# Moving the pool means, their row sums and two scale pieces in the start of a hybrid decoder block

## The chip, the cores and the metric

The kernel runs on one core of a Trainium2 chip. The metric is the device time of one execution in microseconds (us), median of several runs. The engines work side by side, each through its own list of instructions in order: TensorE (PE, with its weight loads shown apart as PEld), VectorE (DVE), ScalarE (ACT), GpSimd (POOL) and SyncE (SP), which here only issues loads.

## The reference

One decoder layer over 1024 tokens of 1024 features. What the change touches is the first half of it:

```python
mod = jax.nn.silu(c) @ w_ada + b_ada
shift1, scale1, gate1, shift2, scale2, gate2 = [m[:, None, :] for m in jnp.split(mod, N_MOD, axis=-1)]
h = rms_norm(x, norm1_pre) * (1.0 + scale1) + shift1
z = h @ w_in
y_a = spatial_gating(z[..., : 2 * D_A], w_spatial, b_spatial, ln_v_gain, ln_v_bias)
y_b = multiscale_pool(z[..., 2 * D_A:], w_pool, b_pool, pool_scale)
mix = jnp.concatenate([y_a, y_b], axis=-1) @ w_out
x = x + gate1 * rms_norm(mix, norm1_post)
```

`multiscale_pool` takes, for each of four groups of 128 features, the mean of the last 2, 4, 8 or 16 tokens (of fewer at the start of the sequence, divided by their true count) minus the token itself, and multiplies the difference by a 128 x 128 matrix. A constant added to every token of a feature drops out of that difference. After this half comes an MLP with a squared ReLU.

## The kernel before

Products in full precision are made of reduced-precision parts (`hi` and `lo`, three products each); a few small ones run in plain float32, which takes two TensorE instructions each. Tokens go in two halves of 512 (h = 0, 1). `start()` does the first half as far as the inputs of the output projection. Its instructions stand in an order written out by hand on all five engines (`manual_schedule`, L1664); from `project` (L1673) to `project_last` a planner puts them in order by its own estimates, and may set them among those of `start()`; the MLP (`expand`, `contract`) is by hand again.

In `start()`, in order:

- **Normalising** (L1391 to L1411). For each of four tiles of 128 tokens: ScalarE squares and sums (`first`), GpSimd takes the power, VectorE scales (`second`), TensorE transposes three of eight feature blocks (`third`).
- **Scale.** The columns of `w_ada` for `scale1` come in five pieces, of 128, 128, 256, 256 and 256 columns. `piece_sum` (L1306) multiplies and adds the eight rows of a piece with `silu(c)` on VectorE into two accumulators, whose sum a ninth step (`both`, L1316) makes. `piece_end` (L1322) adds over the partitions by TensorE products with a column of ones, and `ada_vector` adds the bias on VectorE. The four pieces of `shift1` go the same way later.
- **Pool products** (`pool_pass`, L1417): z of the pool groups without the shift, into the PSUM tiles `pbs`, feature block after feature block; `scaled_hi`, `pool_hi` (ACT) and `scaled_lo`, `pool_lo` (DVE) make the operands. ScalarE copies the result to `zbs` (L1513).
- **Value products** (L1552 to L1586), with the shift pieces beside them. What the shift adds is computed from sums of the weights' rows, weighted by the shift: `row_sum` into `vacc` (value), `uacc` (gate) and `bacc` (pool).
- **Gate products** (`gate_pass`, L1591) with `sums_b` and `sums_u` beside them on VectorE, and the statistics of the values (`values`).
- **Tail** (L1631 to L1661). `row_vector(bacc)` gives the shift of the pool groups, which ScalarE adds to `zbs`; `windowed` (L379) makes the means from it on VectorE and saves the last 16 tokens in `halo` for the second half; `spatial_products`; `pool_out` (L415) multiplies by the pool matrix; `spatial_end` (L470) makes the four `ya`. `stream.fill(n)` takes the next unit of `w_out` (load `w_raw`, ACT `whi`, DVE `wlo`). `load_x(1)` loads the second half's tokens into the tiles that held the pool weights (`braw` is `xs[4]` to `xs[7]`), so each such load waits until `sums_b` has read its tile.

Then `project` (L552) needs the first unit of `w_out` and the first two pool results, four PSUM tiles for four tiles of tokens.

Of the kernel before, what the change touches and what calls it, by code (L numbers as in the profile page):

```python
# [40 lines left out]
def block_kernel(  # L41
# [64 lines left out]

    def load_x(h):
        for i in range(NT):
            nc.sync.dma_start(out=xs[h * NT + i], in_=x[0, (h * NT + i) * P:(h * NT + i + 1) * P, :])
# [9 lines left out]
    ident = const.tile([P, P], F32, name="ident")  # L119
    make_identity(nc, ident)  # L120
    ones = const.tile([P, P], F32, name="ones")
    nc.vector.memset(ones, 1.0)
# [347 lines left out]

    def spatial_end(h, j, ps, u):
        t = tmp.tile([P, NT, P], F32, tag="t", name=f"ya{h}_{j}")
        nc.vector.scalar_tensor_tensor(
            t, ps.rearrange("p (n t) -> p n t", t=P), vec[:, V_LG + j:V_LG + j + 1],
            Bsp[:, j:j + 1, :].broadcast_to([P, NT, P]), ALU.mult, ALU.add,
        )
        tf = t.rearrange("p n t -> p (n t)")
        nc.vector.tensor_tensor(tf, tf, u, ALU.mult)
        y = fact.tile([P, 2, HT], F32R, tag="f", name=f"yas{h}_{j}")
        split(y[:, 0], y[:, 1], tf)  # L480
        return y

# [823 lines left out]
    def piece_sum(blk, c0, n, ts):  # L1306

        def step(kt):
            def run():
                acc = acc_of[blk][kt % 2][:, c0:c0 + n]  # L1310
                if kt < 2:
                    nc.vector.tensor_scalar(acc, ts[kt], silu_c[:, kt:kt + 1], None, ALU.mult)
                else:
                    nc.vector.scalar_tensor_tensor(acc, ts[kt], silu_c[:, kt:kt + 1], acc, ALU.mult, ALU.add)
            return run
        def both():  # L1316
            a, b = [acc_of[blk][o][:, c0:c0 + n] for o in range(2)]
            nc.vector.tensor_tensor(a, a, b, ALU.add)

        return [step(kt) for kt in range(KT)] + [both]  # L1320

    def piece_end(blk, c0, n, split=False):  # L1322
        pa = ps_tile(f"pa{blk}_{c0}")
        nk = n // P
        for k in range(nk):
            at = c0 + k * P
            nc.tensor.matmul(pa[:, k:k + 1], lhsT=acc_of[blk][0][:, at:at + P], rhs=ones[:, 0:1], start=True, stop=True)
        rest = lambda: ada_vector(blk, pa[:, 0:nk], range(c0 // P, c0 // P + nk))
        return rest if split else rest()

# [8 lines left out]
    def start():  # L1339
# [50 lines left out]

        g = piece_sum(1, *PIECES[0], sc[0])  # L1391
        first(0)
        first(1)
        vectors_a()
        second(0)
        third(0)
        first(2)
        second(1)
        third(1)
        first(3)  # L1400
        second(2)
        third(2)
        weave(g)
        second(3)
        scale_rest = piece_end(1, *PIECES[0], split=True)
        third(3)
        scale_rest()
        for i in range(NT):
# [5 lines left out]
        hT = []  # L1414
        pbs = [ps_tile(f"pb0_{j}") for j in range(NG)]

# [16 lines left out]
        hT.append(scaled_hi(pts[0], 0))  # L1433
        g = piece_sum(1, *PIECES[1], sc[1])
        weave(g[:KT // 2])
        scaled_lo(hT[0], pts[0], 0)
        weave(g[KT // 2:])
        pool_lo(0)
        pool_pass(0, 0)
        pool_pass(0, 1)  # L1440
        piece_end(1, *PIECES[1])
        his(1)
        pool_pass(0, 2)
        more(3)
        g = piece_sum(1, *PIECES[2], sc[2])
        weave(g[:KT // 2])
# [17 lines left out]
        def value_hi(kp):  # L1464
            nc.scalar.copy(vw[kp][0], vraw[kp])
# [39 lines left out]
        value_lo(0, 0)  # L1505
        value_lo(0, 1)
        pool_pass(KT - 1, 1)
        pool_pass(KT - 1, 2)
# [10 lines left out]

        bacc, vacc, uacc = rows_of("b"), rows_of("v"), accp.tile([P, 512], F32, tag="junk", bufs=1, name="shift_wu")  # L1520

# [30 lines left out]
        for kp in range(NQ):  # L1552
            if kp == 0:
                sh.append(piece(0, 2 * QC, QC))
                value_tiles(1)
                value_hi(1)
# [25 lines left out]
            if kp == 1:  # L1582
                rest_b()
                turn()
            if kp == 2:
                offsets()  # L1586


# [24 lines left out]
        for i in range(NT):  # L1613
            nc.tensor.matmul(pvs[i], lhsT=ones_r, rhs=vb[:, 0], start=False, stop=False)
            nc.tensor.matmul(pvs[i], lhsT=ones_r, rhs=vb[:, 1], start=False, stop=True)
        weave(sums_b(0, 4), sums_u(0, 2))
        gate_load(3)
        gate_pass(2)
        gate_pass(3)
        steps, vs = values(0, pvs)  # L1620
        weave(steps[:4], sums_b(4, 8))
        gate_hi(2)
        gate_lo(2, 0)
        gate_lo(2, 1)
        gate_pass(4)
        weave(steps[4:], sums_u(2, 6))
# [24 lines left out]
        ya = []  # L1651
        for j in range(NHEAD):
            if j in (1, 2):
                stream.fill(1 + j)
            ya.append(spatial_end(0, j, psp[j], us[j]))
            if j < 2:
                yb[2 + j][1]()
            if j == 2:
                measure()
        apply()  # L1660
        return ya + [y for y, low in yb]  # L1661


    with tc.manual_schedule(engines={E.DVE, E.Activation, E.PE, E.Pool, E.SP}):  # L1664
        y0 = start()
    nxt = {}

    def prepare(key, h, n, name):
        def run():
            nxt[key] = hidden(h, n, name)  # L1670
        return run
# [38 lines left out]
```

## Time and profile before

| | us |
|---|---|
| median of 3 runs | 917.52 |
| lowest, highest | 917.51, 918.11 |
| profiled execution | 918.05 |
| its span, first to last instruction | 916.4 |

TensorE is busy for 97% of the span, VectorE for 75%, ScalarE for 46%, GpSimd for 10%. The profile says for each engine when it worked, what it waited for, and which clock TensorE was granted (1.0 is the upper of two levels). It lists no clock before the first change that it recorded, and shows 1.0 there.

### The profile page before, as it was taken

How to read it: one execution, taken by the hardware profiler on the slowest of the kernel's cores; microseconds unless marked ns; L12 is line 12 of the kernel's file. 1: busy time of each engine (PE TensorE's matmuls, PEld its weight loads, DVE VectorE, ACT ScalarE, POOL GpSimd, SP SyncE). 2: the span in 40 equal slices, each digit the busy share in tenths (PEclk: the TensorE clock that was granted, in tenths of full speed). 3: DMA queues.
4: the chain of work that ended last, by engine and by line, in shares of the span. 5: the costliest groups of instructions: out<-in, count | busy, mean ns of one | idle time of the engine just before them, and what ended most of it. 6: DMA issues, size and time to landing. Idle time of an engine off the chain costs nothing.

```text
span 916.4 us, 10781 instructions
## 1 busy us (share of the span) xinstructions
PE 888.7 (97%) x3960; PEld 723.9 (79%) x3960; DVE 687.5 (75%) x980; ACT 419.1 (46%) x558; POOL 88.8 (10%) x147
## 2 busy tenths in 40 slices
PE   4999999999999999999999999999999999999994
PEld 3788678888887888888888888888888888888883
DVE  5988878799758997766666656477987774569796
ACT  3323675334366665444444354454455433434331
POOL 4001020003003001111100101010000000000032
PEclk9999999999999999999999999999999999999997
DMA  9934356584824159533444434499975884334664
GB/s 309 352 111 149 98 149 199 160 271 151 254 81 151 41 142 303 184 138 132 168 149 157 141 138 148 139 358 392 354 239 196 291 271 123 107 114 139 208 213 153
DMA packets 114105, 173.52 MB, mean 189 GB/s; under 512 B 6098, under 2 KB 61442, under 8 KB 114052
## 3 DMA queue, kind: packets, MB, share of 16 engines
q1 hardware_dynamic: 104292, 135.03, 46.0%
q0 software_dynamic: 9760, 37.80, 10.7%
q8 instruction: 31, 0.51, 0.2%
q14 instruction: 22, 0.18, 0.1%
HBM read 135.06 MB, written 37.75 MB: 189 GB/s over the span
## 4 chain that ended last, share of the span: by engine, by line
PE 59%; issue 32%; DVE 4%; ACT 2%; DMA 2%; POOL 1%; SPq 0%; POOLq 0%; DVEq 0%; ACTq 0%
PE a L828 6%; PE a L829 6%; PE a L830 6%; PE p L830 3%; PE p L828 3%; PE p L829 3%; PE po L86 3%; PE po L87 3%; PE po L85 3%; PE pb L1421 3%; PE pu L1596 2%; PE pv L85 2%; PE pv L87 2%; PE pv L86 2%; PE b L828 2%
## 5 line engine op out<-in xcount | busy, mean ns | idle before, releaser
L85 PE MATMUL m<-thi,shi 128*128 128x512 f32 x448 | 174.3, 389 | 0.0
L86 PE MATMUL m<-tlo,shi 128*128 128x512 f32 x448 | 174.3, 389 | 0.0
L87 PE MATMUL m<-thi,slo 128*128 128x512 f32 x448 | 174.3, 389 | 0.0
L94 DVE TENSOR_TENSOR slo<-s,shi 128x1024 fp32r<-128x1024 f32 x56 | 68.4, 1222 | 58.8 <-ACT shi L91 58.8
L91 ACT CAST shi<-s 128x1024 fp32r<-128x1024 f32 x56 | 59.0, 1053 | 107.3 <-PE m L86 58.1
L87 PEld LDWEIGHTS m<-thi,slo 128*128 128x128 f32 x448 | 84.1, 188 | 17.6
L86 PEld LDWEIGHTS m<-tlo,shi 128*128 128x128 f32 x448 | 84.1, 188 | 17.4
L85 PEld LDWEIGHTS m<-thi,shi 128*128 128x128 f32 x448 | 84.1, 188 | 17.4
L91 ACT CAST thi<-wt 128x1024 fp32r<-128x1024 f32 x40 | 42.1, 1051 | 37.4 <-DVE wt L571 23.7
L91 ACT CAST whi<-w_raw 128x1024 fp32r<-128x1024 f32 x28 | 29.3, 1052 | 53.4 <-DMA w_raw<-in_w_in_dram 15.7
L94 DVE TENSOR_TENSOR tlo<-wt,thi 128x1024 fp32r<-128x1024 f32 x40 | 48.9, 1223 | 1.4
L571 DVE TENSOR_TENSOR wt<-wt,b 128x1024 f32<-128x1024 f32 x32 | 39.1, 1223 | 13.6 <-DMA b<-in_w_fc_dram 11.1
L571 DVE TENSOR_TENSOR S<-c,F 128x1024 f32<-128x1024 f32 x12 | 14.7, 1224 | 38.7 <-ACT F L861 38.7
L94 DVE TENSOR_TENSOR wlo<-w_raw,whi 128x1024 fp32r<-128x1024 f32 x28 | 34.1, 1220 | 7.8 <-ACT whi L91 7.8
L291 POOL TENSOR_TENSOR f<-msf,neg_half 128x1 f32<-128x1 f32 x8 | 7.2, 901 | 282.0 <-DVE msf L1160 282.0
L858 ACT COPY F<-a 128x512 f32<-128x512 f32 x16 | 9.4, 586 | 53.9 <-PE a L830 53.9
L598 ACT CAST hic<-wo 128x1024 fp32r<-128x1024 f32 x16 | 16.8, 1053 | 31.2 <-DVE wo L571 31.2
L181 DVE SCALAR_TENSOR_TENSOR ada_acc<-ada_raw,silu_c,ada_acc 128x1024 f32<-128x1024 f32 x21 | 26.9, 1280 | 3.9 <-DMA ada_raw<-in_w_ada_dram 3.8
L603 DVE TENSOR_TENSOR lob<-wa,hib 128x1024 fp32r<-128x1024 f32 x16 | 19.6, 1225 | 13.4 <-ACT hib L598 13.4
L598 ACT CAST hib<-wa 128x1024 fp32r<-128x1024 f32 x16 | 16.7, 1050 | 25.8 <-DVE wa L571 25.8
L85 PE MATMUL po<-whi,ybs 128*128 128x512 f32 x64 | 25.8, 406 | 1.6 <-ACT yb L419 0.9
L86 PE MATMUL po<-wlo,ybs 128*128 128x512 f32 x64 | 26.2, 410 | 0.0
(311 smaller groups left out, 2194.3 us busy)
## 6 DMA issues: line engine op xcount, KB each, us to landing
s<-fD SPq DMA_DIRECT2D x56, 512.0 KB, 4.2
wt<-in_w_fc_dram SPq DMA_DIRECT2D x40, 512.0 KB, 5.1
ada_raw<-in_w_ada_dram SPq DMA_DIRECT2D x24, 512.0 KB, 4.6
fD<-S POOLq DMA_DIRECT2D x16, 768.0 KB, 3.7
wa<-in_w_fc_dram SPq DMA_DIRECT2D x20, 512.0 KB, 4.0
piece<-in_w_ada_dram SPq DMA_DIRECT2D x16, 512.0 KB, 8.3
w_raw<-in_w_out_dram SPq DMA_DIRECT2D x16, 512.0 KB, 4.6
wo<-in_w_fc_dram SPq DMA_DIRECT2D x16, 512.0 KB, 4.5
```

Source lines behind the costliest of these rows:

```text
L85: nc.tensor.matmul(ps, lhsT=ah, rhs=bh, start=start, stop=False)
L86: nc.tensor.matmul(ps, lhsT=ah, rhs=bl, start=False, stop=False)
L87: nc.tensor.matmul(ps, lhsT=al, rhs=bh, start=False, stop=stop)
L91: nc.scalar.copy(hi, src)
L94: nc.vector.tensor_tensor(lo, src, hi.bitcast(F32), ALU.subtract)
L181: nc.vector.scalar_tensor_tensor(acc, t, silu_c[:, kt:kt + 1], acc, ALU.mult, ALU.add)
L571: nc.vector.tensor_tensor(o, a, b, op)
L598: nc.scalar.copy(unit_tiles(kind, n)[0], src)
L828: nc.tensor.matmul(ps, lhsT=ah, rhs=bh, start=first, stop=False, skip_group_check=not start)
L829: nc.tensor.matmul(ps, lhsT=ah, rhs=bl, start=False, stop=False, skip_group_check=not start)
L830: nc.tensor.matmul(ps, lhsT=al, rhs=bh, start=False, stop=last, skip_group_check=not start)
L1421: nc.tensor.matmul(pbs[j], lhsT=w[:, j * P:(j + 1) * P], rhs=a, start=k == 0 and n == 0, stop=k == KT - 1 and n == 2)
```

## The change

It does seven things. (1) The difference "mean minus token" is made from `zbs` without the shift, so the addition on ScalarE goes; only the saved `halo` gets the shift, in `shift_halo`, which runs just before the second half's hidden features. `row_vector(bacc)` moves there too. (2) `windowed` of groups 0, 1 and 2 moves up, into the value products and the first gate products, and three `pool_out` move in front of the sixth gate product. (3) `sums_b` moves down, behind `sums_u` and in pieces between the `ya`. (4) `load_x(1)` is cut in two: two tiles ahead of `stream.fill(1)`, two behind. (5) The steps that make `ya` are cut, so that their `lo` parts stand later, and the norm of the second half comes after all four. (6) A tile of zeros is set, and `busy(n)` multiplies it by itself, 30 times in all, around the first transposes. (7) The first two scale pieces are summed by TensorE alone (`piece_direct`), and `both` goes: `piece_end` multiplies both accumulators. The second unit of value weights is made ready (`value_hi(1)`) before the last pool products.

```diff
+    idle = tmp.tile([P, 512], BF16, tag="t", name="idle")
+    nc.vector.memset(idle, 0.0)
...
-        split(y[:, 0], y[:, 1], tf)
-        return y
+        nc.scalar.copy(y[:, 0], tf)
+        return y, lambda: nc.vector.tensor_tensor(y[:, 1], tf, y[:, 0].bitcast(F32), ALU.subtract)
...
-        def both():
-            a, b = [acc_of[blk][o][:, c0:c0 + n] for o in range(2)]
-            nc.vector.tensor_tensor(a, a, b, ALU.add)
...
-            nc.tensor.matmul(pa[:, k:k + 1], lhsT=acc_of[blk][0][:, at:at + P], rhs=ones[:, 0:1], start=True, stop=True)
+            for o in range(2):
+                nc.tensor.matmul(pa[:, k:k + 1], lhsT=acc_of[blk][o][:, at:at + P], rhs=ones[:, 0:1], start=o == 0, stop=o == 1)
...
+    def piece_direct(blk, c0, ts):
+        pa = ps_tile(f"pa{blk}_{c0}")
+        for kt in range(KT):
+            nc.tensor.matmul(pa[:, 0:1], lhsT=ts[kt], rhs=silu_c[:, kt:kt + 1], start=kt == 0, stop=kt == KT - 1)
+        return lambda: ada_vector(blk, pa[:, 0:1], range(c0 // P, c0 // P + 1))
...
+        def busy(n):
+            for _ in range(n):
+                nc.tensor.matmul(pbs[0], lhsT=idle[:, 0:P], rhs=idle, start=True, stop=True)
+        busy(12)
         first(0)
         first(1)
         vectors_a()
+        busy(8)
         second(0)
         third(0)
+        busy(2)
         first(2)
         second(1)
         third(1)
+        busy(4)
         first(3)
         second(2)
         third(2)
-        weave(g)
+        scale_rest = piece_direct(1, 0, sc[0])
         second(3)
-        scale_rest = piece_end(1, *PIECES[0], split=True)
         third(3)
+        busy(4)
         scale_rest()
...
         pool_pass(0, 0)
+        piece_direct(1, P, sc[1])()
         pool_pass(0, 1)
-        piece_end(1, *PIECES[1])
...
+        value_tiles(1)
+        value_hi(1)
         pool_pass(KT - 1, 1)
         pool_pass(KT - 1, 2)
...
             if kp == 1:
                 rest_b()
                 turn()
+                weave(windowed(0, 0, zbs[0]))
             if kp == 2:
                 offsets()
+                weave(windowed(0, 1, zbs[1]))
...
-        weave(sums_b(0, 4), sums_u(0, 2))
         gate_load(3)
+        weave(sums_u(0, 2), windowed(0, 2, zbs[2]))
...
+        yb = [pool_out(0, j, pair_of(diffs[0], j)) for j in range(3)]
         gate_pass(5)
-        bvec = row_vector(bacc, "b")
-        for j in range(NG):
-            z = zbs[j][:, HALO:]
-            nc.scalar.activation(z, z, AF.Identity, bias=bvec[:, j:j + 1])
-        weave(sums_u(6, 8), windowed(0, 0, zbs[0]))
+        weave(sums_u(4, 6))
+        yb[0][1]()
+        yb[1][1]()
         gate_pass(6)
+        weave(sums_u(6, 8))
+        bacc = accp.tile([P, 512], F32, tag="acc", name="shift_wb")
+        rest_u = sums_b(0, KT)
+        weave(rest_u[:4])
+        load_x(1, range(2))
+        stream.fill(1)
         gate_pass(7)
         psp = [spatial_products(0, j, vs) for j in range(2)]
         uvec = row_vector(uacc, "u")
         us = [gate(0, j, pus[j], uvec[:, j:j + 1]) for j in range(NHEAD)]
-        weave(windowed(0, 1, zbs[1]), windowed(0, 2, zbs[2]))
         psp += [spatial_products(0, j, vs) for j in range(2, NHEAD)]
-        yb = [pool_out(0, j, pair_of(diffs[0], j)) for j in range(2)]
         weave(windowed(0, 3, zbs[3]))
-        for y, low in yb:
-            low()
-        stream.fill(1)
-        yb += [pool_out(0, j, pair_of(diffs[0], j)) for j in range(2, NG)]
-        load_x(1)
+        stream.fill(2)
+        yb[2][1]()
+        yb += [pool_out(0, 3, pair_of(diffs[0], 3))]
+        weave(rest_u[4:6])
+        yb[3][1]()
+        stream.fill(3)
...
+        def shift_halo():
+            bvec = row_vector(bacc, "b")
+            for j in range(NG):
+                nc.vector.tensor_scalar(halo[:, j, :], halo[:, j, :], bvec[:, j:j + 1], None, ALU.add)
```

## Rows read from the trace of the kernel before

**Rows 1.** The page, parts 1 and 2: busy time; granted clock in 40 slices.
```profile
PE 888.7 (97%) x3960; PEld 723.9 (79%) x3960; DVE 687.5 (75%) x980; ACT 419.1 (46%) x558; POOL 88.8 (10%) x147
...
PEclk9999999999999999999999999999999999999997
```

**Rows 2.** Windows (us): busy time, instructions; then granted clock, DMA share, GB/s.
```profile
16.20:25.00 8.80, 6.96 (x27) 5.25 (x27) 7.56 (x21) 1.20 (x3) 1.13 (x3) 1.00 1.09 359
25.00:72.00 47.00, 47.00 (x225) 37.82 (x225) 41.82 (x101) 14.63 (x23) 1.02 (x5) 1.00 0.67 221
75.14:93.92 18.78, 18.78 (x88) 15.61 (x87) 18.36 (x39) 6.46 (x11) 4.14 (x4) 1.00 0.57 181
104.00:108.10 4.10, 2.28 (x5) 0.78 (x5) 3.49 (x6) 3.95 (x7) 0.00 (x0) 1.00 0.00 0
108.10:111.86 3.76, 3.75 (x10) 2.97 (x11) 3.02 (x5) 2.18 (x3) 0.00 (x0) 0.55 0.46 139
```

**Rows 3.** Timeline (start, duration, instruction, idle before): first pool products, later ones.
```profile
16.25 3.69 PE L1421 MATMUL pb<-ha,wbhi 128*128 128x512 f32 x8 [0.35 <-ACT ha L1333]
...
34.18 2.10 PE L1421 MATMUL pb<-ha,wbhi 128*128 128x512 f32 x8
```

**Rows 4.** Timeline of the start: scale pieces, the fourth token tile, the first wait.
```profile
11.91 0.48 DVE L1312 TENSOR_SCALAR ada_acc<-piece,silu_c 128x128 f32<-128x128 f32 x2
...
14.16 0.62 ACT L1368 CAST wbhi<-x 128x512 fp32r<-128x512 f32 x1 [2.85 <-DMA x<-in_w_in_dram]
14.20 0.75 DVE L1385 TENSOR_SCALAR x<-x,r_a 128x1024 f32<-128x1024 f32 x1
...
20.36 0.61 DVE L1312 TENSOR_SCALAR ada_acc<-piece,silu_c 128x256 f32<-128x256 f32 x2
...
24.52 0.52 PEld L1327 LDWEIGHTS pa<-ones,ada_acc 128*128 128x128 f32 x4 [1.98 <-DVE ada_acc L1318]
```

**Rows 5.** Timeline of weight loads: one-column products, and what follows them.
```profile
31.28 0.64 PEld L1327 LDWEIGHTS pa<-ones,ada_acc 128*128 128x128 f32 x4
31.84 0.77 PEld L1421 LDWEIGHTS pb<-ha,wbhi 128*128 128x128 f32 x4
...
90.15 1.09 PEld L1531 LDWEIGHTS pab<-ones,shift_wb 128*128 128x128 f32 x8
91.16 1.00 PEld L1596 LDWEIGHTS pu<-ha,wuwhi 128*128 128x128 f32 x5
```

**Rows 6.** Timeline of VectorE: group 3 of the pool, first and last of seven.
```profile
100.24 0.17 DVE L384 COPY halo<-zb 128x16 f32<-128x16 f32 x1
...
103.47 0.69 DVE L399 SCALAR_TENSOR_TENSOR diff<-s,zb 128x512 f32<-128x512 f32 x1
```

**Rows 7.** SyncE's issues in order; its waits; the landing of `w_raw` (us).
```profile
77.41 0.38 SPq L242 DMA_DIRECT2D w_raw<-in_w_out_dram  x1
77.83 7.64 SPq L109 DMA_DIRECT2D x<-in_x_dram  x4
...
SPq L109 <- DVE shift_wb L1526: 5.9, 3, 3.1
...
DMA to landing us min/median/max: 3.9/4.5/4.8
```

**Rows 8.** Timeline around the start of the output projection.
```profile
101.23 2.74 PE L417 MATMUL pp<-diff,wpl 128*128 128x512 f32 x6
...
104.31 1.10 PE L417 MATMUL pp<-diff,wpl 128*128 128x512 f32 x2 [0.33 <-DVE diff L399]
...
104.95 1.04 ACT L91 CAST whi<-w_raw 128x1024 fp32r<-128x1024 f32 x1
...
106.03 1.23 DVE L94 TENSOR_TENSOR wlo<-w_raw,whi 128x1024 fp32r<-128x1024 f32 x1 [0.25 <-ACT whi L91]
...
106.05 1.18 PE L85 MATMUL po<-whi,ybs 128*128 128x512 f32 x3 [0.65 <-ACT whi L91]
...
108.11 0.52 PE L85 MATMUL po<-whi,ybs 128*128 128x512 f32 x1 [0.88 <-ACT yb L419]
...
111.84 0.41 PE L85 MATMUL po<-whi,ybs 128*128 128x512 f32 x1
```

**Rows 9.** SyncE's timeline: a load of a later stage.
```profile
40.58 0.33 SPq L174 DMA_DIRECT2D G<-in_norm_post_dram  x1
```

More of the change, by code (lines that the diff above doesn't have):

```diff
@@ L105, in block_kernel, with load_x @@
     rinv = [const.tile([P, NT], F32, name=f"rinv{h}") for h in range(NH)]
-    def load_x(h):
-        for i in range(NT):
+    def load_x(h, tiles=range(NT)):
+        for i in tiles:
             nc.sync.dma_start(out=xs[h * NT + i], in_=x[0, (h * NT + i) * P:(h * NT + i + 1) * P, :])
@@ L471, in spatial_end, with spatial_begun @@
     def spatial_end(h, j, ps, u):
+        y, low = spatial_begun(h, j, ps, u)
+        low()
+        return y
+    def spatial_begun(h, j, ps, u):
         t = tmp.tile([P, NT, P], F32, tag="t", name=f"ya{h}_{j}")
@@ L1315, in step, with piece_end @@
             return run
-        def both():
-            a, b = [acc_of[blk][o][:, c0:c0 + n] for o in range(2)]
-            nc.vector.tensor_tensor(a, a, b, ALU.add)
-        return [step(kt) for kt in range(KT)] + [both]
-    def piece_end(blk, c0, n, split=False):
+        return [step(kt) for kt in range(KT)]
+    def piece_end(blk, c0, n):
         pa = ps_tile(f"pa{blk}_{c0}")
@@ L1326, in piece_end @@
             at = c0 + k * P
-            nc.tensor.matmul(pa[:, k:k + 1], lhsT=acc_of[blk][0][:, at:at + P], rhs=ones[:, 0:1], start=True, stop=True)
-        rest = lambda: ada_vector(blk, pa[:, 0:nk], range(c0 // P, c0 // P + nk))
-        return rest if split else rest()
+            for o in range(2):
+                nc.tensor.matmul(pa[:, k:k + 1], lhsT=acc_of[blk][o][:, at:at + P], rhs=ones[:, 0:1], start=o == 0, stop=o == 1)
+        ada_vector(blk, pa[:, 0:nk], range(c0 // P, c0 // P + nk))
+    def piece_direct(blk, c0, ts):
[3 more added lines that the diff above has]
+        return lambda: ada_vector(blk, pa[:, 0:1], range(c0 // P, c0 // P + 1))
     def scaled_hi(ps, k):
@@ L1389, in third @@
                 nc.tensor.transpose(out=pts[k][:, i * P:(i + 1) * P], in_=xs[i][:, k * P:(k + 1) * P], identity=ident)
-        g = piece_sum(1, *PIECES[0], sc[0])
+        pbs = [ps_tile(f"pb0_{j}") for j in range(NG)]
+        def busy(n):
+            for _ in range(n):
+                nc.tensor.matmul(pbs[0], lhsT=idle[:, 0:P], rhs=idle, start=True, stop=True)
+        busy(12)
         first(0)
@@ L1414, in start @@
         hT = []
-        pbs = [ps_tile(f"pb0_{j}") for j in range(NG)]
         def pool_pass(k, n):
@@ L1433, in start @@
         hT.append(scaled_hi(pts[0], 0))
-        g = piece_sum(1, *PIECES[1], sc[1])
-        weave(g[:KT // 2])
+        g = piece_sum(1, *PIECES[2], sc[2])
         scaled_lo(hT[0], pts[0], 0)
-        weave(g[KT // 2:])
         pool_lo(0)
         pool_pass(0, 0)
+        piece_direct(1, P, sc[1])()
         pool_pass(0, 1)
-        piece_end(1, *PIECES[1])
         his(1)
@@ L1444, in start @@
         more(3)
-        g = piece_sum(1, *PIECES[2], sc[2])
         weave(g[:KT // 2])
@@ L1518, in rows_of @@
             return fact.tile([P, 512], F32, tag="f", name=f"shift_w{n}")
-        bacc, vacc, uacc = rows_of("b"), rows_of("v"), accp.tile([P, 512], F32, tag="junk", bufs=1, name="shift_wu")
+        vacc, uacc = rows_of("v"), accp.tile([P, 512], F32, tag="junk", bufs=1, name="shift_wu")
         def row_sum(acc, k, src):
@@ L1554, in start @@
                 sh.append(piece(0, 2 * QC, QC))
-                value_tiles(1)
-                value_hi(1)
                 gate_load(0)
@@ L1620, in start @@
         steps, vs = values(0, pvs)
-        weave(steps[:4], sums_b(4, 8))
+        weave(steps[:4])
         gate_hi(2)
@@ L1625, in start @@
         gate_pass(4)
-        weave(steps[4:], sums_u(2, 6))
+        weave(steps[4:], sums_u(2, 4))
         gate_hi(3)
@@ L1640, in start @@
         us = [gate(0, j, pus[j], uvec[:, j:j + 1]) for j in range(NHEAD)]
-        weave(windowed(0, 1, zbs[1]), windowed(0, 2, zbs[2]))
         psp += [spatial_products(0, j, vs) for j in range(2, NHEAD)]
-        yb = [pool_out(0, j, pair_of(diffs[0], j)) for j in range(2)]
         weave(windowed(0, 3, zbs[3]))
-        for y, low in yb:
-            low()
-        stream.fill(1)
-        yb += [pool_out(0, j, pair_of(diffs[0], j)) for j in range(2, NG)]
-        load_x(1)
-        measure, apply = normalise(1, "a")
[L1651 to L1659, printed above, removed]
-        apply()
+        stream.fill(2)
[4 more added lines that the diff above has]
+        stream.fill(3)
+        ya = [spatial_begun(0, 0, psp[0], us[0])]
+        weave(rest_u[6:7])
+        ya[0][1]()
+        ya.append(spatial_begun(0, 1, psp[1], us[1]))
+        weave(rest_u[7:8])
+        ya[1][1]()
+        load_x(1, range(2, NT))
+        ya.append(spatial_begun(0, 2, psp[2], us[2]))
+        measure, apply = normalise(1, "a")
+        ya.append(spatial_begun(0, 3, psp[3], us[3]))
+        ya[2][1]()
+        ya[3][1]()
+        measure()
+        apply()
+        ya = [y for y, low in ya]
+        def shift_halo():
+            bvec = row_vector(bacc, "b")
+            for j in range(NG):
+                nc.vector.tensor_scalar(halo[:, j, :], halo[:, j, :], bvec[:, j:j + 1], None, ALU.add)
+        late["halo"] = shift_halo
         return ya + [y for y, low in yb]
+    late = {}
     with tc.manual_schedule(engines={E.DVE, E.Activation, E.PE, E.Pool, E.SP}):
@@ L1669, in run @@
         def run():
+            late["halo"]()
             nxt[key] = hidden(h, n, name)
```

## The prediction

> **What bounds the kernel now.** I read the busy shares first: TensorE works for 888.7 us of 916.4 [rows 1]. So it sets the time, and a gain must come out of its 28 us of pauses or out of stretches at half clock; work added to it in a dense stretch costs in full. The windows then say where the pauses are. From 16.2 to 25 TensorE is busy 6.96 of 8.80; from 25 to 72 it never pauses; from 104 to 108.1 it is busy 2.28 of 4.10; and from 108.1 to 111.86 it is busy but at a granted clock of 0.55 [rows 2]. The rest of its pauses lie before 16 us and in the last 12 us. The change touches the first 25 us and the stretch around 104; I price TensorE's delay ("d", after minus before, minus is earlier) from landmark to landmark.
>
> Two rows show what the start hides. Eight pool products take 3.69 us at 16.25 and 2.10 at 34.18 [rows 3]: the first ran at half clock, although the profile shows 1.0 there. In the page's slices the clock looks full throughout [rows 1]; only the instructions' own times give it away.
>
> **Start, to 25 us.** Before, VectorE does the first scale piece from 11.91 and gets to the fourth token tile at 14.20; the first pool weights land at 14.16, and the pool products start at 16.25 [rows 3, 4]. With `piece_direct`, VectorE loses eight steps and `both`, and the token tile can be scaled at about 12.4, when GpSimd's power is there. TensorE gets 16 instructions, each with a weight load. Eight such loads stand 1.01 us apart from what follows, four 0.56 [rows 5]: 0.11 to 0.14 each, so 2.0 us at full clock. Third transposes done at 12.5, direct sum to 14.5, fourth transposes, bias on VectorE, `scaled_hi` (ScalarE is free at 14.8, after the cast at 14.16): pool products from 15.9 instead of 16.25. Little is won here, since the weights land no sooner. Four of them 0.9, the second direct sum 2.0 (to 18.8), then VectorE takes the bias at 19.3 and starts the third piece, 1.05 us ahead of the 20.36 of before [rows 4]. That lead carries through: the one-column products of that piece start about 23.05 instead of 24.52, but take 0.9 instead of 0.45. d = -1.0.
>
> The zeros: if they bring the clock up before 12 us and it stays, the above holds. 12 at half clock last 5 us (half the rate of [rows 3]), from 1.2 to at most 6.4; the other 18 fit between the transposes at 0.23 each, as those wait for VectorE.
>
> **25 to 72 us, dense.** `piece_end` now makes 8 products where it made 4, for two more scale pieces and four shift pieces. From [rows 5], 0.4 us more each, six times: +2.4. `both` leaves VectorE, but no wait of TensorE on VectorE of any size stands in this stretch [rows 2], so that gives at most 0.1. d = +1.3 (+0.6 to +1.9). Here the Trainium skill would have it cheaper: "TensorE: Matmul & The Clock Gate", section "Wait — 56ns, not 53.3ns?", puts the floor between small products at about 25 ns, by which the 24 added instructions cost 0.6 us and d is -0.5. The rows decide: each product has weights of its own, and 0.11 to 0.14 us is what they stand apart.
>
> **Gate products and tail.** From TensorE the row vector of `bacc` (1.0 us, [rows 5]) goes, to come back later; three pool products come in, 6 x 0.457 = 2.75 [rows 8]. So it is through the spatial products, and at the fourth `pool_out`, at 101.1 + 1.3 - 1.0 + 2.75 = 104.2.
>
> Is that product's input there? VectorE: the window of group 3 takes from 100.24 to 104.16, 3.9 us [rows 6]; of groups 0, 1, 2 by their fewer steps of 0.73: 1.75, 2.45 and 3.2. Groups 0 and 1 now stand in the value stage (+4.2), three `both` leave it (-1.0), and VectorE's pauses there (`value_hi` earlier, the wait for the last shift piece) swallow about 1.1: VectorE reaches the sums 2.1 late (1.2 to 3), at 77.2 instead of 75.14. From 75.14 to 93.92 it did, densely (18.36 of 18.78, [rows 2]), sixteen row sums less a few steps, the values and their parts: 18.7. Now the same without four sums (4 x 0.66 = 2.65), with group 2 (3.2) and two `lo` (1.2): 20.4. So the fourth `sums_b` ends at 97.5.
>
> **The queue.** On SyncE the two loads of x now stand ahead of the first `w_raw`. Before, `w_raw` went at 77.41, ahead of the x loads, which waited on `sums_b` for 5.9 us [rows 7]. Now `x5` can't be issued before 97.5, and `w_raw`, which needs nothing of that, goes behind it at 98.0. It takes 3.9 to 4.8 us to land [rows 7]; with two loads in front 4.3: 102.3. Then `whi` 1.04 and `wlo` 1.15 [rows 8], and `wlo` stands on VectorE in front of the window of group 3: that starts at 104.5 and ends at 108.4. Behind the waiting `whi` on ScalarE stand the gates, which don't suffer (TensorE's row sums come at 102.5).
>
> So TensorE waits at the fourth `pool_out` from 104.2 to 108.4, 4.2 us (2.2 to 5.5: `sums_b` a microsecond sooner or later, landing 3.8 to 4.9). In the rows before, 1.8 us of gaps between 104 and 108.1 were followed by a stretch at 0.55 that took 1.7 us [rows 2]; after a longer gap I take 1.4 (0 to 1.7). [...]
>
> **The sum.** Before, the thirteenth product of the projection starts at 111.84 [rows 8]. After: 108.4 + 0.92 (the pool product) + 12 x 0.233 + 1.4 = 113.5, d = +1.7. Then the row vector of `bacc` comes back before the second half's transposes (+1.0), and gaps of some 0.3 near 129, where the fourth `ya` was late, go. VectorE's four additions to `halo` and the later x loads lie beside products. d = +2.4, and what follows is dense. The profiled execution took 918.05 for a span of 916.4; its own forecast is 920.4, and against the median of 917.52 I forecast **919.9**, own range 917.3 to 922.
>
> **Rivals.**
> - *The tail closes (faster).* If TensorE does not stand at the fourth product, the whole loss of before goes: from 101.1 to 111.84 it needed 4 x 0.92 + 12 x 0.233 = 6.5, so 4.3 was lost. Then the projection's thirteenth product is at 104.2 + 3.7 = 107.9, d = -3.9, +1.0 - 0.3, and some 0.5 back because VectorE, with the last `sums_b` between the `ya`, delivers the fourth late: 914.9. The mechanism is the planner: it may set the projection's products before the waiting one, as it set the load of G, which belongs to a later stage, at 40.58 among the hand-ordered loads [rows 9]. It decides from about 12 products (2.8 us) put there once `wlo` is ready. Against it: of eight PSUM tiles the spatial products hold four and the fourth pool product needs one, so at most three of four token tiles could go first; and before, no projection product stands ahead of a pool product [rows 8]. A VectorE that is 4 us quicker than I reckon does the same.
> - *A short wait.* With 2 us of wait and no fall of the clock, d is about -1: 916.6.
> - *The clock does not hold through the start.* At half clock the direct sums take 4 us each (as [rows 3], twice as long) and the zeros stand in front of the transposes: the pool products start some 2 us later, on top of the forecast: 921.9. At 108.1 the clock was low although TensorE had worked more than half of the 4 us before [rows 2]; between 6 and 12 us it works about as much.
>
> **How the numbers follow.** The forecast gets 0.45, the closed tail 0.35, the short wait 0.10, the lost clock 0.10. Range 914.6 to 922.2: below lies a third of the second case, above a tenth of the first and some of the last. About 0.2% (1.8 us) is what measurements can tell from no change: the forecast's lower part (0.15), most of the short wait (0.08) and a little of the rest (0.06) make 0.29 for the same; faster 0.32 (0.30 of the closed tail); slower 0.39.
>
> **What would show it.** Right: TensorE's longest wait after 25 us is at L417's counterpart for `diff` near 104 to 108; SyncE issues `w_raw` near 98 behind x; VectorE is idle for some 5 us before `wlo`; eight weight loads at each `piece_end`; pool products near 16 at 0.23 each. Wrong: projection products before the fourth pool product, `w_raw` issued near 77, or pool products still at 0.46 each.

## The result and the profile after

The changed kernel takes 923.80 us (median; 922.44 to 925.08) against 917.82 for the kernel before: a ratio of 1.0074, interval 1.0062 to 1.0085. It is slower by some 6 us, as forecast in sign, but 1.6 us above the range. Executions of one kernel lie up to 3.8 us apart (number 9 below; the kernel before in the later measurements: 915.7 to 918.2), so below the medians size an effect and the traces, one execution each, show its place. The profiled execution took 924.98 us for a span of 922.7, against 918.05 and 916.4.

The page, busy time and granted clock, to hold beside [rows 1]:

```profile
PE 902.0 (98%) x4046; PEld 734.6 (80%) x4046; DVE 681.8 (74%) x960; ACT 416.8 (45%) x554; POOL 88.3 (10%) x147
...
PEclk9999799999999999999999999999999999999998
```

The slices already show it: one of them, 92 to 115 us, has fallen from 9 to 7. The windows (columns as in [rows 2]) say more:

```profile
16.20:25.00 8.80, 8.53 (x54) 7.09 (x52) 6.82 (x20) 2.96 (x6) 0.56 (x2) 1.00 1.09 359
25.00:72.00 47.00, 47.00 (x236) 38.49 (x235) 40.57 (x97) 12.61 (x20) 0.83 (x5) 1.00 0.66 215
...
104.00:108.00 4.00, 1.98 (x8) 1.68 (x8) 3.86 (x7) 3.23 (x5) 0.00 (x0) 0.50 0.76 272
108.00:112.00 4.00, 2.98 (x5) 1.78 (x6) 3.93 (x6) 0.86 (x2) 0.00 (x0) 0.50 0.19 55
112.00:116.00 4.00, 4.00 (x14) 3.15 (x14) 3.24 (x5) 2.43 (x3) 0.00 (x0) 0.75 0.69 219
...
136.00:140.00 4.00, 3.10 (x19) 3.05 (x20) 4.00 (x11) 2.54 (x7) 3.67 (x5) 0.74 0.49 136
```

The start lost its pauses: TensorE is busy 8.53 of 8.80 us from 16.2 to 25, where it was 6.96 [rows 2]. From 104 to 114 TensorE has both pauses and the lower clock (0.50, that is 1.2 GHz), and the clock falls once more near 138. Before, only 108.5 to 111.9 was slow.

TensorE in the start (timeline; to hold beside [rows 3, 4]):

```profile
1.26 4.49 PE L1406 MATMUL pb<-idle 128*128 128x512 bf16 x12 [1.26 <-DVE idle L122]
...
15.04 1.20 PE L1440 MATMUL pb<-ha,wbhi 128*128 128x512 f32 x4
16.08 1.84 PE L1338 MATMUL pa<-silu_c,piece 128*128 128x1 f32 x16
...
21.53 1.23 PE L1331 MATMUL pa<-ones,ada_acc 128*128 128x1 f32 x8 [0.26 <-DVE ada_acc L1321]
```

Four pool products now take 1.20 us and start at 15.04; the eight of [rows 3] took 3.69 from 16.25. The third piece's column products start at 21.53 instead of 24.52 [rows 4]. So the start gained more than I gave it: 2.4 us.

The tail, queue by queue. SyncE (to hold beside [rows 7]):

```profile
95.26 1.90 SPq L109 DMA_DIRECT2D x<-in_x_dram  x2
97.25 13.15 SPq L244 DMA_DIRECT2D w_raw<-in_w_out_dram  x6
...
123.08 0.34 SPq L109 DMA_DIRECT2D x<-in_x_dram  x1
```

ScalarE and VectorE, which wait for that load (to hold beside [rows 6, 8]):

```profile
102.74 1.04 ACT L91 CAST whi<-w_raw 128x1024 fp32r<-128x1024 f32 x1 [9.64 <-DMA w_raw<-in_w_out_dram]
```

```profile
94.44 2.33 DVE L1544 SCALAR_TENSOR_TENSOR shift_wb<-x,shift,shift_wb 128x512 f32<-128x512 f32 x3
103.82 1.23 DVE L94 TENSOR_TENSOR wlo<-w_raw,whi 128x1024 fp32r<-128x1024 f32 x1 [7.05 <-ACT whi L91]
...
108.18 0.69 DVE L401 SCALAR_TENSOR_TENSOR diff<-s,zb 128x512 f32<-128x512 f32 x1
```

And TensorE, which waits for both (to hold beside [rows 8]):

```profile
103.90 2.08 PE L470 MATMUL psp<-wcT,vs 128*128 128x128 f32 x8 [1.53 <-ACT vecu L1551]
109.02 2.05 PE L419 MATMUL pp<-diff,wpl 128*128 128x512 f32 x2 [3.05 <-DVE diff L401]
```

`w_raw`, issued at 77.41 before, goes out at 97.25 behind `x4` and `x5`. VectorE stands still for 7.05 us between its fourth row sum and `wlo`, with the window of group 3 queued behind; ScalarE for 9.64 us, with the row vector of the gates queued behind. TensorE loses 1.53 and 3.05 us to them, and the clock.

The last place is before the transposes of the second half. These wait for the norm of its tokens, whose squares ScalarE makes. In the kernel before, the squares stood behind the third `ya` and the transposes did not wait:

```profile
121.98 1.06 ACT L308 ACTIVATE junka<-x 128x1024 bf16<-128x1024 f32 x1
...
131.86 3.65 PE L324 MATMUL pta<-ident,x 128*128 128x128 f32 x32
```

Now (ScalarE's first and last square, then VectorE, then TensorE):

```profile
128.56 1.05 ACT L310 ACTIVATE junka<-x 128x1024 bf16<-128x1024 f32 x1
...
133.58 1.06 ACT L310 ACTIVATE junka<-x 128x1024 bf16<-128x1024 f32 x1
```

```profile
134.84 1.28 DVE L183 SCALAR_TENSOR_TENSOR ada_acc<-ada_raw,silu_c,ada_acc 128x1024 f32<-128x1024 f32 x1 [1.44 <-DMA ada_raw<-in_w_ada_dram]
...
136.04 0.14 DVE L298 TENSOR_SCALAR msa<-ssa 128x1 f32<-128x1 f32 x1
136.10 2.73 DVE L319 TENSOR_SCALAR x<-x,r_a 128x1024 f32<-128x1024 f32 x4
```

```profile
134.70 0.95 PE L1549 MATMUL pab<-ones,shift_wb 128*128 128x1 f32 x8
...
136.90 5.39 PE L326 MATMUL pta<-ident,x 128*128 128x128 f32 x32 [1.26 <-DVE x L319]
```

Part (5) of the change puts the squares behind the fourth `ya`, whose cast on ScalarE starts at 128.03. From there ScalarE works without a pause, with other work between the squares, and never waits for a load of x, although `x7` is issued as late as 123.08. The last square is ready at 134.74. VectorE takes its mean only at 136.04, because a step of another sum stands ahead and waits 1.44 us for its own load (`ada_raw`). The transposes wait 1.26 us and then take 5.39 instead of 3.65.

### The profile page after: what moved, and what is told of

The parts are those of the page before. It is cut to its first block, busy times and chain, and to the rows that moved or that the text cites. A ratio compares the mean times of both kernels' runs of the same rounds, so it can differ in the third digit from the quotient of the medians.

```text
span 922.7 us, 10934 instructions
## 1 busy us (share of the span) xinstructions
PE 902.0 (98%) x4046; PEld 734.6 (80%) x4046; DVE 681.8 (74%) x960; ACT 416.8 (45%) x554; POOL 88.3 (10%) x147
## 4 chain that ended last, share of the span: by engine, by line
PE 57%; issue 31%; DVE 6%; DMA 3%; POOL 1%; ACT 1%; SPq 0%; POOLq 0%; DVEq 0%; ACTq 0%
PE a L835 6%; PE a L836 6%; PE a L837 6%; PE p L837 3%; PE p L835 3%; PE p L836 3%; PE po L85 3%; PE po L86 3%; PE po L87 3%; PE pb L1440 2%; PE pv L85 2%; PE b L835 2%; PE b L836 1%; PE pv L87 1%; PE b L837 1%
```

## The experiments

Theory A: the order on SyncE. A load that needs nothing stands behind loads that wait for row sums; all of the loss follows from that. Theory B: TensorE's added work (the doubled column products, the row vector that comes back before the transposes). Twelve kernels, in three groups of four, each group measured beside the kernel before. "Place" is where the second half's pool products begin against the kernel before (158.11 us there, 164.51 in the changed one), in the profiled execution.

| kernel | median us | before us | ratio (interval) | place, us |
|---|---|---|---|---|
| changed | 923.80 | 917.82 | 1.0074 (1.0062 to 1.0085) | +6.40 |
| 1 w_raw ahead of x | 916.53 | 916.95 | 0.9996 (0.9987 to 1.0005) | -2.69 |
| 2 casts later | 918.38 | 916.95 | 1.0019 (1.0010 to 1.0028) | +0.87 |
| 3 wait filled | 921.05 | 916.95 | 1.0045 (1.0032 to 1.0059) | +2.89 |
| 4 single ends | 922.99 | 916.95 | 1.0067 (1.0054 to 1.0080) | +4.94 |
| 5 before + start | 913.84 | 916.64 | 0.9976 (0.9965 to 0.9987) | -4.24 |
| 6 x6, x7 early | 922.63 | 916.64 | 1.0065 (1.0052 to 1.0078) | +3.16 |
| 7 = 1 + single ends | 914.67 | 916.64 | 0.9979 (0.9969 to 0.9990) | -3.32 |
| 8 = 7 + tail reordered | 916.81 | 916.64 | 1.0003 (0.9994 to 1.0012) | +0.27 |
| 9 before + zeros | 916.95 | 916.67 | 1.0002 (0.9993 to 1.0011) | +0.44 |
| 10 = 5 without zeros | 920.28 | 916.67 | 1.0038 (1.0026 to 1.0051) | +2.76 |
| 11 = 5 + cast early | 913.15 | 916.67 | 0.9966 (0.9955 to 0.9976) | -4.98 |
| 12 = 5 + x first | 914.05 | 916.67 | 0.9972 (0.9961 to 0.9982) | -4.50 |

**1. Only SyncE's order.**

```diff
-        load_x(1, range(2))
         stream.fill(1)
+        load_x(1, range(2))
```

> Against the changed kernel only SyncE's order differs: the first w_raw load stands ahead of the x4 and x5 loads again. Theory A (queue order: the load of w_raw waited behind x loads that wait for VectorE's row sums): w_raw is issued near 77 us, whi and wlo are done before 99 us, TensorE's waits of 3.0 us before the fourth pool_out and 1.5 us before the last spatial products go, the granted clock stays at 1.0 from 100 to 116 us, VectorE is 5 to 7 us earlier with its last four sums, x7 is issued by 118 us instead of 123.1, and the wait of 1.3 us with the second fall of the clock at 138 us goes too: 913 to 917 us. Theory B (TensorE's own added work, the 24 added one-column products and the moved row vector, is what costs): the time stays at 922 to 925 us.

SyncE, TensorE and two windows of it:

```profile
76.76 0.38 SPq L244 DMA_DIRECT2D w_raw<-in_w_out_dram  x1
94.82 1.91 SPq L109 DMA_DIRECT2D x<-in_x_dram  x2
```

```profile
102.69 1.02 PE L419 MATMUL pp<-diff,wpl 128*128 128x512 f32 x2
```

```profile
104.00:108.00 4.00, 4.00 (x19) 3.21 (x18) 3.38 (x5) 3.75 (x5) 0.00 (x0) 1.00 0.52 167
108.00:112.00 4.00, 4.00 (x19) 3.22 (x18) 4.00 (x6) 1.05 (x1) 0.00 (x0) 1.00 0.74 260
```

Two swapped lines take the slowdown from 6.0 us to nothing (0.4 us under before, not measurable). Both waits and the half clock are gone, as A said, and B falls as the main cause. Of A's details one missed: `x7` was issued at 116.5 as expected, but 1.03 us of wait before the transposes stayed. So that wait does not come from the lateness of `x7`.

**2. The order as changed, but the casts that wait are issued behind the window of group 3.**

```diff
-        split(hi, lo, t)
+        if n == 1:
+            late["split"] = lambda: split(hi, lo, t)
+        else:
+            split(hi, lo, t)
...
         weave(windowed(0, 3, zbs[3]))
+        late["split"]()
```

> SyncE's order is that of the changed kernel, so w_raw still lands near 102.3 us; only the two casts that wait for it (whi on ScalarE, wlo on VectorE) are issued behind the window of group 3. Theory A, in the form that the harm is what is queued behind the waiting casts: the window ends near 101 us, the fourth pool_out follows the spatial products without a wait, the projection starts near 105 us: 915 to 919 us. Rival (the late landing of w_raw itself holds the projection): the wait moves to the first projection product and the time stays above 921 us. Theory B: 922 to 925 us.

```profile
103.33 1.02 PE L422 MATMUL pp<-diff,wpl 128*128 128x512 f32 x2
105.24 0.97 PE L85 MATMUL po<-whi,ybs 128*128 128x512 f32 x3 [0.89 <-ACT whi L91]
106.50 0.50 PE L86 MATMUL po<-wlo,ybs 128*128 128x512 f32 x1 [0.29 <-DVE wlo L94]
```

4.5 us of the 6.0 come back although `w_raw` is as late as ever (issued at 97.48). So the larger part of the harm is what was queued behind the two casts; the late load itself holds the projection by 0.89 and 0.29 us.

**3. Products of ready data in TensorE's wait.**

```diff
+        if (h, j) == (0, 3):
+            for _ in range(11):
+                nc.tensor.matmul(ps, lhsT=ones_r, rhs=late["fill"], start=True, stop=True)
         nc.tensor.matmul(ps, lhsT=wpl[:, j], rhs=d, start=True, stop=True)
...
+        late["fill"] = uw[3][0][:, 0]
```

> The changed kernel with 11 products of ready data (128x512, overwritten by the real one) ahead of the fourth pool_out, in TensorE's wait. The wait itself stays: the fourth pool_out near 109 us. If the clock's fall is a cost of its own, the granted clock is back at 1.0 by 109 to 110 us instead of 114.0 and the time is 2.0 to 2.5 us below the changed kernel's in the same job. If the wait alone cost the time, no difference (within 0.5 us).

```profile
105.75 4.06 PE L421 MATMUL pp<-wuwhi,ones_r 128*128 128x512 f32 x11
109.64 1.04 PE L422 MATMUL pp<-diff,wpl 128*128 128x512 f32 x2
...
110.75 0.40 PE L86 MATMUL po<-wlo,ybs 128*128 128x512 f32 x1
```

The pool product is no sooner (109.64), the projection's follow each other at 0.23 us instead of 0.43, and 1.9 us come back between the medians against before: the clock's fall is a cost of its own, about a third of the loss. (In the traces it is 3.5 us, because in this one the second fall, at the transposes, is missing too.)

**4. Single column products again, VectorE adding the halves.**

```diff
+        def both():
+            a, b = [acc_of[blk][o][:, c0:c0 + n] for o in range(2)]
+            nc.vector.tensor_tensor(a, a, b, ALU.add)
...
-            for o in range(2):
-                nc.tensor.matmul(pa[:, k:k + 1], lhsT=acc_of[blk][o][:, at:at + P], rhs=ones[:, 0:1], start=o == 0, stop=o == 1)
+            nc.tensor.matmul(pa[:, k:k + 1], lhsT=acc_of[blk][0][:, at:at + P], rhs=ones[:, 0:1], start=True, stop=True)
```

> The changed kernel with the pieces' ends as before: VectorE adds the two halves of a piece and TensorE takes one product for each column, 24 fewer in six groups. Theory B, and the step of the prediction that priced them at 2.4 us: 2.3 to 2.6 us below the changed kernel if what comes behind moves with them; theory A alone: TensorE reaches the wait before the fourth pool_out 2.5 us earlier and only waits longer, so the time differs by less than 1 us.

```profile
105.14 2.08 PE L470 MATMUL psp<-wcT,vs 128*128 128x128 f32 x8 [4.24 <-ACT vecu L1554]
```

No difference to the changed kernel in the medians (6.04 against 5.98 us over before): TensorE comes 1.5 us earlier and waits 4.24 us instead of 1.53 at the same place. B has no price as long as that wait stands. There are seven groups of column products, the third piece's among them, and so 28 TensorE instructions fewer, at 0.45 us a group 3.2 us; I had counted 24 in six. The 1.5 is less than that because this execution lost some 1.6 us in the start: 0.7 before its first pool products, the rest where products ran at half rate (four take 1.91 us from 20.00). I first read that as VectorE's addition holding the third piece (its column products begin at 23.35 instead of 21.53), and kept two products there in 7; but TensorE shows no wait for VectorE at that place.

**5. The kernel before with the new start alone** (zeros, two scale pieces on TensorE, products moved up, the third piece with two products for a column; tail as before).

> The kernel before with the start of the changed one alone: zeros first, two scale pieces on TensorE, pool products moved up, the third piece with two products for a column; everything from the second pass of products on, and the whole gate and tail, as before. The start's step: the ninth group of pool products begins 2.0 to 2.6 us earlier than before (27.28 us), as in the changed kernel (24.9). If the tail of the kernel before lets it through: 914.8 to 915.6 us, 1.5 to 2 us under before. If VectorE's windows hold the fourth pool_out there (they end last before it in the kernel before): the gain shrinks to under 0.8 us, 916.2 to 917.

```profile
101.61 1.10 PE L419 MATMUL pp<-diff,wpl 128*128 128x512 f32 x2 [0.34 <-DVE diff L401]
103.36 1.18 PE L85 MATMUL po<-whi,ybs 128*128 128x512 f32 x3 [0.65 <-ACT whi L91]
105.42 0.50 PE L85 MATMUL po<-whi,ybs 128*128 128x512 f32 x1 [0.89 <-ACT yb L421]
```

2.8 us faster than before, and a microsecond under what I had expected. In the trace TensorE is 2.69 us earlier up to the tail, with the same three pauses as in [rows 8]; but the stretch at 0.55 that followed them [rows 2] is missing, which gives another 1.55. That part I had not foreseen, and these traces don't show why it came (last section). (The medians show 2.8 of these 4.2 us; the kernel before has shorter executions than its profiled one.)

**6. Row sums five to eight left out, x6 and x7 loaded early.**

```diff
-        weave(rest_u[4:6])
+        load_x(1, range(2, NT))
...
-        weave(rest_u[6:7])
...
-        weave(rest_u[7:8])
...
-        load_x(1, range(2, NT))
```

> The changed kernel without the last four row sums of the pool weights (the shift's row vector for the halo lacks four of eight rows: a part of the computation is left out), and with the loads of x6 and x7 right behind x5 and the first w_raw loads. SyncE's order at w_raw is that of the changed kernel, so the 3.0 us and 1.5 us waits near 104 to 109 us and the half clock there stay. Theory: the late x loads (x7 issued at 123.1 us) are a second cost of their own; with them early, the 1.3 us wait before the second half's transposes and the fall of the clock at 138 us go: 2 to 3.5 us under the changed kernel, 920.5 to 922. Rival (late x loads lie beside products, as the prediction had it): within 0.7 us of the changed kernel.

```profile
134.94 3.73 PE L326 MATMUL pta<-ident,x 128*128 128x128 f32 x32
...
138.50 1.28 DVE L183 SCALAR_TENSOR_TENSOR ada_acc<-ada_raw,silu_c,ada_acc 128x1024 f32<-128x1024 f32 x1
```

Undecided. In the trace the wait before the transposes and their half clock are gone and the place is 3.2 us better; the median is not (5.99 us over before, as the changed kernel's 5.98). Two of the changed kernel's four executions were 2.5 us shorter than the profiled one, at 922.4 and 922.6, which is where this one lies. So the second loss may belong to some executions only; what of it the median holds stays open. Nor does the trace bear out the theory that late loads of x are the cost: ScalarE's squares run behind the fourth `ya` here as well (127.55 to 133.9), without a wait for x in either kernel. What differs is that VectorE, without four row sums, is 1.0 us earlier with the fourth `ya` (its cast starts at 127.02 instead of 128.03), and that the step of the other sum stands behind the scaling of x (138.50 instead of 134.84). A kernel that moves that step alone was not run.

**7. Number 1 with single ends in six of the seven groups.** (Its diff is that of 1, and that of 4 except for the third piece.)

> The first experiment's order of SyncE (w_raw ahead of x4 and x5) and, in five of the six groups of column products, VectorE's addition of the halves and single products again; the third piece, where VectorE's addition held the start back in the fourth experiment, keeps two. TensorE is 2.0 to 2.2 us earlier at the spatial products than in the first experiment. If TensorE bounds the tail: 2 us under the first experiment, 914.4 us. If VectorE does (its last window ended 1.4 us before the fourth pool_out in the first experiment, and it was busy without a pause from 104.6 to 121.6 us): 0.3 to 1.3 us under it, 915.3 to 916.2.

```profile
100.92 1.10 PE L419 MATMUL pp<-diff,wpl 128*128 128x512 f32 x2 [0.43 <-DVE diff L401]
```

TensorE is 2.4 us earlier at the spatial products than in 1 and then waits: 0.43 for the window, 1.03 for a pool output's activation. Between medians against before 1.6 us are left, between the two cases; 0.35 of it lies outside of the span (last section). Against 5 this kernel differs only in what stands behind the start, and it is 0.8 us slower, with intervals that overlap: the rearranged tail, its order mended, brings nothing that can be measured.

**8. Number 7 with VectorE's order changed in the tail and the squares of x issued tile by tile.**

```diff
         weave(windowed(0, 3, zbs[3]))
+        yb[2][1]()
+        weave(rest_u[4:6])
         stream.fill(2)
-        yb[2][1]()
...
-        weave(rest_u[4:6])
...
+        load_x(1, [2])
...
+        measured(range(3))
         ya.append(spatial_begun(0, 3, psp[3], us[3]))
```

> The seventh experiment, and in the tail VectorE's fifth and sixth row sums and a low half go ahead of the second w_out cast, into the 3.25 us in which VectorE waited for whi there; x6 is loaded before the seventh and eighth sums instead of behind them; the squares and scalings of x4 to x6 don't wait for x7. Theory (VectorE and the late x loads bound this tail once SyncE's order is right): x6 issued near 104 us, x7 by 114 us, no wait before the second half's transposes, 1 to 2 us under the seventh: 913.3 to 914.8. Rival (TensorE's own work bounds it): no difference from the seventh.

`measured(range(3))` issues the squares of `x4` to `x6` ahead of the last `ya`. TensorE, then VectorE:

```profile
126.47 0.80 PE L87 MATMUL po<-whi,yas 128*128 128x512 f32 x1 [3.11 <-DVE yas L488]
```

```profile
120.25 0.15 DVE L298 TENSOR_SCALAR msa<-ssa 128x1 f32<-128x1 f32 x1 [1.74 <-ACT junka L1668]
122.41 0.75 DVE L181 TENSOR_SCALAR ada_acc<-ada_raw,silu_c 128x1024 f32<-128x1024 f32 x1 [2.00 <-DMA ada_raw<-in_w_ada_dram]
```

2.1 us slower than 7 between the medians, instead of 1 to 2 faster (the profiled execution lies 1.5 us above its median). The x loads did come early (`x6` issued at 103.45), but now a small step that waits for a square, and a sum's step that waits for its load, stand on VectorE ahead of the last `ya`: the fault of the change made again, on another queue.

**9. The kernel before with the zeros alone.**

```diff
+        busy(12)
         first(0)
...
+        busy(8)
         second(0)
...
```

> The kernel before with the zero products alone; the first two scale pieces stay on VectorE. The fifth experiment gained 2.7 us at the ninth group of pool products (27.28 us before). If the clock alone makes that gain: 2 us or more of it here. If VectorE's two piece sums hold the start (its third sum began at 20.36 us in the kernel before): under 1 us of it here. In time: 915.0 to 916.5 us against 913.8 of the fifth.

```profile
14.52 0.38 PE L1329 MATMUL pa<-ones,ada_acc 128*128 128x1 f32 x2 [1.74 <-DVE ada_acc L1320]
...
23.33 0.61 PE L1329 MATMUL pa<-ones,ada_acc 128*128 128x1 f32 x4 [1.55 <-DVE ada_acc L1320]
23.80 1.99 PE L1433 MATMUL pb<-ha,wbhi 128*128 128x512 f32 x4
```

No gain (0.3 us over before). The clock is up early, but TensorE waits 3.3 us for VectorE's piece sums, and behind the second wait the products run at half rate again (1.99 us for four).

**10. Number 5 without the zeros.**

> The fifth experiment without its 30 zero products and their memset: two scale pieces on TensorE, pool products moved up, half clock until TensorE's own work raises it (19.7 us in the kernel before). If zeros and pieces add up: what the ninth experiment leaves of the 2.7 us, 1 to 2 us of it. If the pieces alone do it, all of it and 913.8 us; if the 32 one-column products at half clock cost what VectorE saves, nothing of it and 916 us or more.

```profile
12.62 3.41 PE L1336 MATMUL pa<-silu_c,piece 128*128 128x1 f32 x16
...
17.26 2.08 PE L1428 MATMUL pb<-ha,wbhi 128*128 128x512 f32 x4 [0.48 <-ACT ha L1341]
```

3.6 us slower than before: the third case, and worse than I had it. Sixteen one-column products take 3.41 us instead of 1.84, and four pool products 2.08 instead of 1.20. Zeros 0.3, pieces 3.6, both together minus 2.8: each pays only with the other.

**11. Number 5 with the first `whi` cast ahead of the gates' row vector on ScalarE.**

```diff
+        stream.fill(1)
         uvec = row_vector(uacc, "u")
...
-        stream.fill(1)
+        late["lo"]()
```

> The fifth experiment with the first w_out cast (whi, 1.04 us) moved on ScalarE from between the pool outputs to its 5.4 us wait before the row vector of the gates; wlo stays where it is on VectorE. TensorE waited 0.65 us for whi and 0.89 us for a pool output's activation behind it. If these two waits are on the path: 1.0 to 1.6 us under the fifth, 912.2 to 912.9. If what is next late (wlo, or the last window) takes their place: within 0.4 us of the fifth.

```profile
102.36 1.44 PE L85 MATMUL po<-whi,ybs 128*128 128x512 f32 x3
```

(`late["lo"]` is `wlo`, which stays in its place.) 913.15 us, the fastest: 3.5 us under before, and 0.7 under 5, with intervals that overlap. The 0.65 us wait for `whi` is gone; the one for the activation keeps its 0.89, since ScalarE has no pause from the gates (97.06) to the last pool output (105.3).

**12. Number 5 with all x loads ahead of `w_raw`.**

```diff
+        load_x(1)
         stream.fill(1)
...
-        load_x(1)
```

> The fifth experiment with all four x loads ahead of the first w_raw load on SyncE, the order that cost the changed kernel; here the row sums that the x loads wait for are done early (the four x loads went out between 75 and 83 us). If the harm lies in the waits of the loads in front and not in the order itself: w_raw is issued by 87 us, lands long before its cast (102.3 us), and the time is within 0.5 us of the fifth. If the order itself costs (2 MB of x in front of the weights): w_raw lands late, TensorE waits for whi before the projection, 1 us or more above the fifth.

```profile
73.78 8.76 SPq L109 DMA_DIRECT2D x<-in_x_dram  x4
82.64 8.85 SPq L244 DMA_DIRECT2D w_raw<-in_w_out_dram  x4
```

0.2 us from 5 (intervals overlap): the same order of loads costs nothing where the row sums that x waits for are done early. What cost 6 us was the lateness of what the loads in front waited for.

## Why the prediction was right and wrong

The sign and the mechanism held: the load of `w_raw` behind the loads of x, and the work behind its casts, make TensorE wait in the tail. The sum failed. In the traces it is +6.4 instead of +2.4, and the step that failed is its last one, "what follows is dense": the wait before the second half's transposes and the low clock in them were put at nothing and measured 1.26 and 1.74 us, of which 0.4 came back (+2.6). The norm, which part (5) moved behind the fourth `ya`, had been given only its gain near 129 and no cost. The other 1.6 are mis-sized terms of the tail: when the load has landed and is cast (+0.6), and the low clock behind the wait (+0.9). The medians (+6.0) need not split in the same way, since the profiled execution of the kernel before is one of its longer ones.

- *Start, d = -1.0: too little.* It came out at -2.4 (the fourth group of pool products at 22.62 instead of 24.99). The third transposes were done 0.4 us sooner than I had them, and the direct sums took 1.84 us, not 2.0, overlapping their neighbours by some 0.15: pool products at 15.04, not 15.9; third piece on VectorE at 18.23, not 19.3. The gain did not reach the end: VectorE and SyncE set the end of the wait. Alone (5) it does. That zeros hold the clock was right, and 9 and 10 add what I had not asked: neither half of the start pays alone.
- *25 to 72 us, +2.4: right.* TensorE goes from -2.4 to +0.2, and never pauses. The rows' 0.11 to 0.14 us for a column product stand (16 in 1.84 us here). The 25 ns that the Trainium skill states as a floor ("TensorE: Matmul & The Clock Gate", "Wait — 56ns, not 53.3ns?") would, taken as the spacing, give an estimate of 0.6 us; the trace lies well above that floor, which sets no upper bound.
- *`both` gives at most 0.1: not contradicted.* With the addition back (4) TensorE shows no wait for it.
- *The queue: right.* Fourth `sums_b` at 96.8 (97.5 said), `w_raw` at 97.25 (98.0), `wlo` after 7.05 us of idling, longest wait of TensorE at `diff`; 1 and 2 confirm the mechanism. The landing was mis-sized: 5.5 us, not 4.3. With 0.1 more in the casts (`wlo` takes 1.23 in [rows 8], I took 1.15) and an issue 0.75 earlier, that puts the pool product at 109.02, not 108.4 (+0.6). TensorE's two waits add up to 4.58 us, against the 4.2 forecast for one.
- *"Behind the waiting `whi` stand the gates, which don't suffer": wrong.* The copy of their row vector frees the PSUM tile that the last spatial products need: 1.53 us of wait. It cost little by itself, since TensorE had to wait for `diff` anyway, but it put the pause earlier, and the clock was at 0.50 before the long wait began.
- *Clock, 1.4: too little.* The twelve products after the wait took 5.02 us instead of 2.80, so 2.2 (+0.8), the pool product 1.06 instead of 0.92 (+0.1). The thirteenth starts at 115.10, not 113.5.
- *Row vector +1.0, gap near 129 -0.3: right.* Measured 0.95 and -0.4.
- *"What follows is dense": wrong in the profiled execution, and the largest miss there.* The fourth `ya` sets when the squares begin, these and a step of another sum on VectorE set when x is scaled, and the transposes wait 1.26 us and lose 1.74 to the clock; 0.4 comes back later. The later loads of x, which I had put beside products, are not the cause: ScalarE never waits for them there. In 1, 2, 3, 4 and 7 a wait of 0.46 to 2.01 us stands at the same place, with `x7` issued anywhere from 116.3 to 123.9 and the same step of VectorE ahead of the last mean. With the 1.6 from the tail that is the whole difference between +2.4 and +6.4. How much of it the median holds, 6 left open.
- *Rivals.* The planner put no projection product ahead of the waiting one, so the tail did not close. The mended order alone (1) gives 916.53, not that rival's 914.9; that 7 comes out at 914.67 is chance, since it has single ends besides. The short wait did not come either (its own sum is -1.2, not -1). The clock held in the start. (The slices of [rows 1] are not full throughout, as I wrote: the last shows 7, in a stretch that the change does not touch.) Theory B's term, real in 25 to 72 us, costs 1.6 us once the wait is gone (7 against 1), and nothing before that (4).

## What to carry to other kernels

Before a load is moved in an in-order queue, ask what the loads ahead of it wait for, not what it waits for itself, and follow that through each queue: DMA issue, cast, the work behind the cast, the PSUM tile that this work frees. An edit in several parts may pay only as a whole (zeros and pieces) or only in one part (start against tail), so time the parts alone and undo them singly. Before a late load is blamed for a wait, look whether the engine that uses it waited for it: ScalarE never waited for x. If an engine will wait anyway, work saved on it upstream is worth nothing until the wait is gone.

## What the runs showed of the hardware

- The same pauses don't always bring the clock down. In the kernel before, waits of 0.33, 0.65 and 0.88 us were followed by a granted clock of 0.55 [rows 2, 8]; in number 5 the same three, 2.69 us earlier, were followed by full clock:

```profile
104.90:108.70 3.80, 3.28 (x14) 2.69 (x15) 3.02 (x5) 2.66 (x4) 0.00 (x0) 1.00 0.42 138
```

  12 (3.0 us early) and 11 (2.5 us early, without the second wait) stayed at full clock, 9 and 10 (0.4 and 2.8 us late) fell. What decides it these traces don't show.
- The same load lands sooner or later. The first `w_raw` (512 KB) took 3.2 us when it went alone (76.76 in number 1) and 5.5 us with two x loads right ahead of it and two more `w_raw` loads within a microsecond behind it (97.25 in the changed kernel); which of these neighbours counts, these traces don't separate. The fit in the Trainium skill ("DMA: Bandwidth & Descriptors", "Anatomy of one DMA — SWDGE (gpsimd) path"), an estimate of 3.2 us for 512 KB, is made for loads issued by GpSimd; these go out from SyncE, and the first agrees with it and the second does not.
- Time outside of the span: 2.0 to 2.1 us in nearly all executions of the changed kernel and of 1, 2, 3 and 6, which have two products for a column in all seven groups; 1.65 to 1.8 in the others. The cause of these 0.35 us was not looked for.
